# A hybrid attention and delta-rule layer on one core: the next block's inputs made ahead of the last projection, the delta rule's decode after the sixth head, two buffers for gate z

## The chip, the core and the metric

The kernel runs on one core of one Trainium2 chip. The metric is the device time of one execution in microseconds (us). Before the change it is 2385.31 us, the median of three runs (2379.32 to 2391.11). The profile is of one more execution, which took 2384.44 us; its span, from the first to the last instruction, is 2382.5 us.

Five engines work in parallel: TensorE (PE: matrix products and transposes; PEld is its loading of the stationary operand), VectorE (DVE), ScalarE (ACT), GpSimd (POOL) and SyncE (SP), which here only issues DMA transfers. ACT issues some transfers too. Each engine runs its instructions in the order in which they stand in its own queue, and an instruction that waits holds up everything behind it.

## The reference

One inference step of one layer, for two sequences: a prompt of 2048 rows of width 1024 with no past, and a sample of 8 sequences of 16 new rows with a cache of 512 past rows each. All in float32.

```
shift, scale, gate = split(silu(c) @ W_ada + b_ada)          # per sequence
h = LN0(x) * (1 + scale) + shift
[qA|kA|vA|gA | qkvB|zB|aB|bB | mA|mB] = h @ W_in             # widths 512 x 8, 4, 4, 1024, 1024
A = differential attention(4 heads, block-causal, relative bias) * silu(gA)
B = gated delta rule(4 heads, causal short conv on q/k/v, RMSNorm * silu(zB))
y = (sigmoid(mA) * (A @ W_pA) + sigmoid(mB) * (B @ W_pB)) @ W_out
x <- LN(alpha * x + gate * y) * ln_g + ln_b
```

Besides the new x it returns the new k and v rows, the last three rows ahead of the convolution and the final delta state (128 x 128 per head), for prompt and sample each. The sample's attention runs over its cache, its delta rule starts from a given state.

## The kernel before

**Phases.** The prompt is cut in four blocks of 512 rows. Phase one goes through 16 steps, one for each block b and head h; the sample's 128 rows ride along with block 0. Phase two then forms y and the new x in five blocks of 512, 512, 512, 384 and 256 rows, the last of which ends with the sample's 128. Between the phases A, B and the merge gates go through DRAM (`ascr`, `tscr`).

**Products in two halves.** Each float32 operand of the large products is split into a high part, a copy in the fast type, and a low part, the difference. A projection (`proj`, all products at L146) makes 128 columns of `h @ W_in` for a block as 24 products: eight slices k of the width with (whi, hhi), eight with (whi, hlo), eight with (wlo, hhi), into one PSUM tile of the pool `pp`, which has two buffers. A projection's result is taken out of `pp` by ACT, and by DVE for the gates, into tiles that often come from the pool `u` (six buffers); a merge gate's tile `tm` (L1378) goes to `tscr` by a transfer at L1380. The two halves of h fill the pool `h`, 16 buffers, so the next block's halves can only be written when the old block's last projection has read theirs. Weights come through the pool `w`, six buffers of 512 KB; they are split once, kept in DRAM (`wscr`) and loaded as pairs from then on, in the order of a list `order`. `split_n(n)` at the start of projection n also fetches n+1 and n+2.

**Four streams.** The program is written by four generators: `gates` (decays and betas of a block), `gdn` (the delta rule), `attention`, and `bulk` (the projections and, at the end, phase two). `plan` interleaves them by modelled due times: a generator gives up its turn with a delay, or with a key that another one must have signalled. After that `arrange` orders each engine's queue anew with a list scheduler over all instructions, with modelled durations. On TensorE products that read `hhi` or `hlo` are set back by 100 us (`AHEAD`), so that transposes, attention and delta rule go first when they are ready and projections fill the rest. Transfers on SP are ordered by when their readers are due; in the first 50 us of modelled TensorE time by their place in the program. Tiles of a pool are given out in program order.

**One step of bulk** is: three projections for attention (`a_proj`: k, q, v), the first merge gates, one more, the two gates of the head (`gate_proj`: g for attention, z for the delta rule, each in a pool with one buffer), the remaining merge gates, and the three delta-rule projections of the next step (`b_proj`: k, q, v with the convolution, into `kq`, two buffers, and `vT`). Gate z's buffer is freed by the last instruction of the head's delta rule (`norm_gate`, L885).

**The edge between blocks.** At the last head of a block, after `gate_proj`, `next_rows` (L404 on) loads the first 512 columns of the next 512 rows into pool `a`, and normalises them on DVE (L228). After the last merge gate `make_h` loads the other 512 columns into pool `u`, and `half_h` makes for each of the eight column slices four transposes into a `pp` tile (L150), the scaling into a `u` tile `h32` (ACT L421 or DVE L419 in turns), the high part on DVE (L401) and the low part on POOL (L402). The row statistics were made one head earlier by `block_stats`.

**The start.** `c` is loaded on SP; its tanh (L242), the transposes and the copy `cT` (L247) lead to `modulation(n)` for n = 0, 2, 1, 3. Each takes eight loads of `w_ada`, 256 KB apiece, on SP (L260) into pools `g` and `a`, eight float32 products into 32 columns each, a copy of the row on DVE (L264) and 16 small products. The x rows of block 0 and the sample, ten loads of 256 KB (L272), and the small set-up loads are issued by ACT.

**Decode and gate rows.** The sample's delta rule (`gdn_decode`) runs in the `gdn` stream after step `GD = (2, 2)` and takes ten tiles of the pool `g`, all of it. The sample's attention (`attn_decode`) runs four times, after the steps in `AD`, for two sequences each time; for each head it transposes 512 cached keys, copies them to `kTd` (pool `wt`, two buffers, L1306) and multiplies them with 32 stationary columns. `gate_rows`, the last third of `W_ada` (16 loads of 256 KB into `u`, at L260), stands at the end of bulk with the twelve small stores of the convolution's last rows (L1421), ahead of phase two, whose first loads are those of `ascr` (L1458) and whose first products are on `ahi` and `alo`.

Of the kernel before, what the change touches and what calls it, by code (L numbers as in the profile page):

```python
# [21 lines left out]
P = 128  # L22
# [3 lines left out]
BLK = 512  # L26
# [17 lines left out]
BUFS = dict(g=10, e=10, wt=2, ao=2, u=6, vT=2, z=1, gg=1, a=5, vv=4, k4=6, kq=2, xc=2, h=16, w=6)  # L44
# [52 lines left out]
GD = (2, 2)  # L97
# [9 lines left out]
GO = 1  # L107
LS = 2.0
# [5 lines left out]
def layer_kernel(  # L114
# [134 lines left out]
    def wide_c():  # L249
        cw_ = tl("wt", "cw_", (P, KD, 32))  # L250
        V.memset(cw_, 0.0)
        V.tensor_copy(cw_[:, :, 0:9], cT)
        return cw_
# [15 lines left out]
    for n in range(5):  # L269
        xt0.append([tl("e", "x0"), tl("e", "x1")])  # L270
        for u in range(2):
            nc.scalar.dma_start(xt0[n][u], rows_of(0, n)[:, u * 512:(u + 1) * 512])  # L272
# [34 lines left out]
    def setup_gates():  # L307
        wab = tl("ao", "wab", (P, KD, 8))
        nc.scalar.dma_start(wab, W[:, C_AB:C_AB + 8].rearrange("(k p) c -> p k c", p=P))
# [4 lines left out]
        nc.scalar.dma_start(nexa, a_log[0:1, :].to_broadcast([P, H]))  # L314
        S.activation(nexa, nexa, AF.Exp)
        V.tensor_scalar(nexa, nexa, -1.0, None, ALU.mult)
        nc.scalar.dma_start(dtb, dt_bias[0:1, :].to_broadcast([P, H]))
        cwr = tl("vv", "cwr", (P, P))[:48]
        nc.scalar.dma_start(cwr, conv_w[0].rearrange("j (n p) -> (j n) p", p=P))
# [4 lines left out]
        nc.scalar.dma_start(ng, Cd("neg"))  # L324
# [12 lines left out]
    def setup_attn():  # L337
        lamv = tl("vv", "lamv", (P, 4, 64))
        for n, a in enumerate((lam_q1, lam_k1, lam_q2, lam_k2)):
            nc.scalar.dma_start(lamv[:, n, :], a[0:1, :].to_broadcast([P, 64]))  # L340
# [11 lines left out]
        nc.scalar.dma_start(subw, subln_w.rearrange("o c -> c o"))  # L352
        V.tensor_scalar(subw, subw, 0.5 * (1.0 - LAM_INIT), None, ALU.mult)
        nc.scalar.dma_start(dnw, dn_norm_w.rearrange("o c -> c o"))
# [3 lines left out]
        nc.scalar.dma_start(rtab, rel_table)  # L358
        oh = tl("vv", "oh")[:32, :384]
        nc.scalar.dma_start(oh, Cd("onehot", 32))  # L360
# [43 lines left out]
    def next_rows(b, u):  # L404
        xs = [tl("au"[u], "xr") for _ in range(4)]
        for n in range(4):
            nc.sync.dma_start(xs[n], rows_of(b, n)[:, u * 512:(u + 1) * 512])
        for n in range(4):
            ln_apply(xs[n], *stats[b], n)
        return xs  # L410

    def half_h(b, u, hhi, hlo, xs):
        for k in range(4 * u, 4 * u + 4):
            pt = (ps_t, ps_pp)[k % 2]() if b == 0 else ps_pp()
# [3 lines left out]
            if k % 2 and b:  # L418
                V.tensor_scalar(h32, pt, modT[:, 8 + k, 0:1], modT[:, k, 0:1], ALU.mult, ALU.add)  # L419
            else:  # L420
                S.activation(h32, pt, AF.Identity, bias=modT[:, k, 0:1], scale=modT[:, 8 + k, 0:1])  # L421
            halves(h32, hhi[k][:, :512], hlo[k][:, :512], V if b == 0 and k % 2 else G)
# [46 lines left out]
    mcol = lambda ms: [(C_MA, C_MB)[w] + m * P for w, m in ms]  # L469
    order += bcol(0)  # L470
    for si, (b, h) in enumerate(steps):
        order += acol(h) + mcol(m_alpha[b, h] + m_beta[b, h][:GO]) + gcol(h) + mcol(m_beta[b, h][GO:])
        if si + 1 < len(steps):
            order += bcol(steps[si + 1][1])
# [21 lines left out]
    def fetch(n):  # L496
        if n < len(order) and n not in raws and n not in pairs:
            if order[n] in kept:
# [35 lines left out]
    def proj(b, evac):  # L534
# [5 lines left out]
        for si, (t0, n) in enumerate([(0, 320), (320, 320)] if b == 0 else [(0, 512)]):  # L540
            pa = ps_pp()
            q = 0
            for w_, x_ in ((whi, hhi), (whi, hlo), (wlo, hhi)):
                for k in range(KD):
                    T.matmul(pa[:, :n], lhsT=w_[:, k, :], rhs=x_[k][:, t0:t0 + n], start=(q == 0), stop=(q == 23))
                    q += 1
                    if q % 4 == 0 and q < 24:
                        yield
                    if q == 4 and si == 0:
# [1381 lines left out]
```

## Time and profile before

| | |
|---|---|
| median of three runs | 2385.31 us (2379.32 to 2391.11) |
| profiled execution, its own time | 2384.44 us |
| its span | 2382.5 us |
| PE busy | 2268.2 us, 95% |
| DVE, ACT, POOL busy | 1479.0, 857.6, 325.5 us |
| mean granted TensorE clock | 0.971 |
| DMA | 537.61 MB, 226 GB/s in the mean |

How to read it: busy time is the union of an engine's instructions. Where PE is granted half the clock, the same product is busy for about twice the time, so a stage loses time both by idle PE and by a clock below 1. "Idle before" with an arrow names what an instruction waited for, as far as semaphores show it.

### The profile page before, as it was taken

The page shows a single profiled execution, that of the slowest core. Times are in us where ns is not written, and L with a number is a line of the kernel's source. Part 1 is how long each engine was busy: PE and PEld are TensorE (multiplying, and loading weights), DVE is VectorE, ACT ScalarE, POOL GpSimd, SP SyncE. Part 2 cuts the span into 40 slices and gives each one's busy share as a digit, 9 for nine tenths or more (in the row PEclk, how much of TensorE's full clock was granted, in tenths as well). Part 3 has the DMA queues.
Part 4 walks back from the last instruction along what each step waited for, and adds up shares of the span by engine and source line. Part 5 has one row for each costly group of instructions (what it writes and reads, how often), then busy time and mean ns, then how long its engine had stood idle before and what let it go on. Part 6 is the DMA issues. An engine that isn't in the chain of part 4 may idle for free.

```text
span 2382.5 us, 41070 instructions
## 1 busy us (share of the span) xinstructions
PE 2268.2 (95%) x14228; PEld 1891.9 (79%) x14228; DVE 1479.0 (62%) x4765; ACT 857.6 (36%) x2604; POOL 325.5 (14%) x696
## 2 busy tenths in 40 slices
PE   4999999999999998999999989989999989999997
PEld 3899999967877786688888776877888766888886
DVE  4645566645655557476658784766777555467467
ACT  1344453533443424353534443534444431000000
POOL 0110120212020101120110022011012011110100
PEclk8899999999999998999999999999999988999999
DMA  8487787957676877375575856636364767797797
GB/s 280 120 268 219 234 267 225 293 176 215 201 249 194 272 229 267 113 231 179 187 239 184 266 174 201 235 97 211 125 216 149 232 202 265 251 358 270 285 376 271
DMA packets 314496, 537.61 MB, mean 226 GB/s; under 512 B 50903, under 2 KB 164079, under 8 KB 314288
## 3 DMA queue, kind: packets, MB, share of 16 engines
q1 hardware_dynamic: 299296, 511.99, 65.7%
q10 hardware_dynamic: 14992, 22.99, 2.8%
q8 instruction: 113, 1.85, 0.3%
q14 instruction: 95, 0.78, 0.1%
HBM read 381.73 MB, written 127.97 MB: 214 GB/s over the span
## 4 chain that ended last, share of the span: by engine, by line
PE 84%; DMA 8%; DVE 3%; SPq 2%; ACT 1%; issue 1%; POOL 0%; ACTq 0%; DVEq 0%; POOLq 0%
PE pp_t L146 51%; PE t_t L146 13%; PE g_t L146 8%; PE v_t L146 7%; PE t_t L150 4%; DMA ql<-lo 2%; DMA wa<-in_w_ada_dram 1%; PE g_t L150 1%; SPq L1061 1%; PE pp_t L150 1%; DMA kst<-lo 1%; DMA tscr<-tm 1%; DMA kscr<-kst 1%; DMA kld<-kscr 0%; DMA wlo<-wscr_m 0%
## 5 line engine op out<-in xcount | busy, mean ns | idle before, releaser
L146 PE MATMUL pp_t<-hhi,whi 128*128 128x512 f32 (+1 forms) x1920 | 467.0, 369 | 7.5 <-ACT tm L1378 3.3
L146 PE MATMUL pp_t<-hlo,whi 128*128 128x512 f32 (+1 forms) x1920 | 464.3, 367 | 0.0
L146 PE MATMUL pp_t<-hhi,wlo 128*128 128x512 f32 (+1 forms) x1920 | 462.3, 367 | 0.0
L146 PEld LDWEIGHTS pp_t<-hhi,whi 128*128 128x128 f32 x1920 | 328.2, 189 | 54.6 <-ACT xc L673 4.6
L146 PEld LDWEIGHTS pp_t<-hhi,wlo 128*128 128x128 f32 x1920 | 328.9, 189 | 44.8 <-issue 4.5
L146 PEld LDWEIGHTS pp_t<-hlo,whi 128*128 128x128 f32 x1920 | 327.0, 189 | 42.3 <-issue 3.9
L1175 DVE TENSOR_REDUCE nm<-t_t 128x1 f32<-128x512 f32 (+3 forms) x256 | 149.1, 591 | 124.6 <-PE t_t L146 121.0
L1182 ACT ACTIVATE e<-t_t,nm 128x512 f32<-128x512 f32 (+3 forms) x256 | 155.5, 610 | 91.4 <-DVE nm L1175 85.6
L1483 ACT ACTIVATE mhi<-th 128x512 fp32r<-128x512 f32 (+2 forms) x40 | 22.7, 568 | 334.5 <-DVE th L1481 129.0
L486 DVE TENSOR_TENSOR wlo<-wraw,whi 128x1024 fp32r<-128x1024 f32 (+1 forms) x80 | 80.6, 1010 | 76.0 <-PE pp_t L146 25.4
L655 DVE SCALAR_TENSOR_TENSOR y<-xc,cw,y 128x512 f32<-128x512 f32 x144 | 107.8, 748 | 1.0
L1216 DVE SCALAR_TENSOR_TENSOR e<-e,f 128x512 f32<-128x512 f32 (+3 forms) x196 | 106.7, 575 | 0.1
L146 PE MATMUL v_t<-vld,wt 128*128 128x128 f32 x768 | 105.0, 280 | 0.0
L146 PEld LDWEIGHTS v_t<-vld,wt 128*128 128x128 f32 x768 | 99.9, 195 | 5.1 <-ACT wt L1225 0.7
L1225 ACT COPY wt<-t_t 128x512 f32<-128x512 f32 (+2 forms) x96 | 51.1, 532 | 141.2 <-PE t_t L150 116.3
L402 POOL TENSOR_TENSOR lo<-k,hi 128x512 fp32r<-128x512 f32 x16 | 20.7, 1292 | 577.6 <-DVE hi L401 270.3
L770 POOL TENSOR_TENSOR tm<-lb,tb 32x15 f32<-32x15 f32 (+7 forms) x255 | 73.7, 289 | 167.8 <-DMA lb<-lscr 147.3
L150 PE MATMUL t_t<-cst,e 128*128 128x128 f32 x544 | 90.3, 277 | 4.5 <-DVE e L1216 4.5
L1462 POOL TENSOR_TENSOR alo<-araw,ahi 128x512 fp32r<-128x512 f32 (+2 forms) x40 | 46.1, 1164 | 324.1 <-DVE ahi L1460 213.8
L146 PE MATMUL t_t<-kld,qh 128*128 128x512 f32 x192 | 80.1, 423 | 8.9 <-DMA kld<-kscr 4.4
L772 POOL TENSOR_TENSOR tb<-tb,tm 32x15 f32<-32x15 f32 (+7 forms) x255 | 82.2, 322 | 19.5
L485 ACT ACTIVATE whi<-wraw 128x1024 fp32r<-128x1024 f32 (+1 forms) x80 | 70.0, 885 | 40.5 <-PE pp_t L146 38.9
(490 smaller groups left out, 4212.2 us busy)
## 6 DMA issues: line engine op xcount, KB each, us to landing
whi<-wscr SPq DMA_DIRECT2D x144, 512.0 KB
wlo<-wscr SPq DMA_DIRECT2D x144, 512.0 KB
wraw<-in_w_in_dram SPq DMA_DIRECT2D x48, 512.0 KB
wscr<-whi SPq DMA_DIRECT2D x48, 512.0 KB
wscr<-wlo SPq DMA_DIRECT2D x48, 512.0 KB
whi<-wscr_m SPq DMA_DIRECT2D x40, 512.0 KB
wlo<-wscr_m SPq DMA_DIRECT2D x40, 512.0 KB
woh<-wscr_o SPq DMA_DIRECT2D x36, 512.0 KB
```

What stands on the lines that cost most here:

```text
L146: return nc.tensor.matmul(out, lhsT=lhsT, rhs=rhs, **kw)
L150: return nc.tensor.transpose(out, in_, identity)
L485: S.activation(whi, r, AF.Copy)
L486: V.tensor_tensor(wlo, in0=r, in1=whi, op=ALU.subtract)
L655: V.scalar_tensor_tensor(y, in0=x_(j), scalar=taps(j), in1=y, op0=ALU.mult, op1=ALU.add)
L770: G.tensor_tensor(tm[:, :n, :j + 1], in0=bc(lb[:, j, j + 1:], j + 1), in1=tb[:, j:j + 1, :j + 1].to_broadcast([32, n, j + 1]), op=ALU.mult)
L772: G.tensor_tensor(tb[:, j + 1:, :j + 1], in0=tb[:, j + 1:, :j + 1], in1=tm[:, :n, :j + 1], op=ALU.subtract)
L1175: V.tensor_reduce(nm[:, c, n:n + 1], sp[:, sl], AX, ALU.max, negate=True)
L1182: S.activation(et[:, sl], src, AF.Exp, bias=nm[:, c, n:n + 1], accum_out=ls[:, c, n:n + 1])
L1216: V.scalar_tensor_tensor(e1[:, sl], in0=e2[:, sl], scalar=coef(1, n), in1=e1[:, sl], op0=ALU.mult, op1=ALU.add)
L1225: (S.copy if kb % 2 == 0 else V.tensor_copy)(wt[:, :w], pt[:, :w])
L1462: G.tensor_tensor(lo, in0=raw, in1=hi, op=ALU.subtract)
```

## The change

1. **The start.** The x loads move from ACT to SP, behind the weights of `modulation(0)`; the small set-up loads move from ACT to SP.
2. **The edge.** `next_h` takes the place of `next_rows` and of half of `make_h`. Ahead of the last merge-gate projections it loads eight column tiles of 512 rows x 128 columns (into five buffers of `a`, two of `xc`, one of `u`), normalises each in four pieces, transposes them, and lets ACT write the scaled result back into the same tile. `make_h`, after the last projection, only copies the high part (ACT) and subtracts (DVE). The first projection of all, and the last of each block and the first of the next, take their 24 products slice by slice.
3. **The gate rows.** `gate_rows` moves from the end of phase one to step (3, 1), between a merge gate and `gate_proj`. Its weights are four entries in `order`, each two tiles of 512 KB of the pool `w`, and it uses `pp`. The convolution's last rows stay at the end (`halo_rows`).
4. **The delta rule's decode** runs after step (1, 2) and no longer after (2, 2).
5. **Buffers.** `z` has two, `u` has five.
6. **The cache decode.** Keys of two heads are transposed and copied before the two products with them are issued, one behind the other.
7. `make_gates` issues its products with `hhi` and `hlo` slice by slice.

```diff
-BUFS = dict(g=10, e=10, wt=2, ao=2, u=6, vT=2, z=1, gg=1, a=5, ...)
+BUFS = dict(g=10, e=10, wt=2, ao=2, u=5, vT=2, z=2, gg=1, a=5, ...)
-GD = (2, 2)
+GD = (1, 2)
+GR = (3, 1)
...
-        for u in range(2):
-            nc.scalar.dma_start(xt0[n][u], rows_of(0, n)[:, u * 512:(u + 1) * 512])
+    def first_rows():
+        for n in range(5):
+            for u in range(2):
+                nc.sync.dma_start(xt0[n][u], rows_of(0, n)[:, u * 512:(u + 1) * 512])
...
-        nc.scalar.dma_start(wab, W[:, C_AB:C_AB + 8].rearrange("(k p) c -> p k c", p=P))
+        nc.sync.dma_start(wab, W[:, C_AB:C_AB + 8].rearrange("(k p) c -> p k c", p=P))
...
+    def next_h(b):
+        mv, r = stats[b]
+        xs = []
+        for k in range(KD):
+            x_ = tl("aaaaaxxu"[k].replace("x", "xc"), "xk")
+            nc.sync.dma_start(x_.rearrange("p (n c) -> p n c", c=P),
+                              x_rows[b * BLK:(b + 1) * BLK, k * P:(k + 1) * P].rearrange("(n p) c -> p n c", p=P))
+            xs.append(x_)
+        for k, x_ in enumerate(xs):
+            pt = ps_pp()
+            for n in range(4):
+                ln_apply(x_[:, n * P:(n + 1) * P], mv, r, n)
+                T.transpose(pt[:, n * P:(n + 1) * P], x_[:, n * P:(n + 1) * P], ident)
+            S.activation(x_, pt, AF.Identity, bias=modT[:, k, 0:1], scale=modT[:, 8 + k, 0:1])
+            yield HH
+        return xs
...
-    def make_h(b, x0):
-        hts[b] = new_h()
-        x1 = next_rows(b, 1)
-        yield from half_h(b, 0, *hts[b], x0)
-        yield from half_h(b, 1, *hts[b], x1)
+    def make_h(b, xs):
+        hts[b] = hhi, hlo = new_h()
+        for k in range(KD):
+            S.activation(hhi[k][:, :512], xs[k], AF.Copy)
+            V.tensor_tensor(hlo[k][:, :512], in0=xs[k], in1=hhi[k][:, :512], op=ALU.subtract)
...
+                pairs[n] = [tl("w", "wa2", (P, 2, 512)) for _ in range(2)]
+                for i, wa in enumerate(pairs[n]):
+                    nc.sync.dma_start(wa, w_ada[0][(k + 2 * i) * P:(k + 2 * i + 2) * P, (4 + u) * 512:(5 + u) * 512].rearrange("(k p) c -> p k c", p=P))
...
+            products = [(w_, x_, k) for w_, x_ in ((whi, hhi), (whi, hlo), (wlo, hhi)) for k in range(KD)]
+            if n0 in edges:
+                products = [products[8 * p + k] for k in range(KD) for p in range(3)]
...
-                kT = tl("wt", "kTd")
-                S.copy(kT, pt)
+                kTs.append(tl("wt", "kTd"))
+                S.copy(kTs[h], pt)
                 yield 1.0
-                q_ = qz[:, h, bi].rearrange("p c t -> p (c t)")
-                T.matmul(sp[32 * h:32 * h + 32, :], lhsT=q_, rhs=kT, start=True, stop=True)
+                if h % 2 == 0:
+                    continue
+                for g in (h - 1, h):
+                    q_ = qz[:, g, bi].rearrange("p c t -> p (c t)")
+                    T.matmul(sp[32 * g:32 * g + 32, :], lhsT=q_, rhs=kTs[g], start=True, stop=True)
...
+            if (b, h) == GR:
+                yield from gate_rows()
             yield from gate_proj(b, h)
             if h == H - 1 and b + 1 < NBLK:
-                x0 = next_rows(b + 1, 0)
+                xs = yield from next_h(b + 1)
...
-        yield from gate_rows()
+        yield from halo_rows()
```

More of the change, by code (lines that the diff above doesn't have):

```diff
@@ L351, in setup_attn @@
         V.tensor_tensor(lamd, in0=lamd, in1=C("cc")[:, 0:1], op=ALU.add)
-        nc.scalar.dma_start(subw, subln_w.rearrange("o c -> c o"))
+        nc.sync.dma_start(subw, subln_w.rearrange("o c -> c o"))
         V.tensor_scalar(subw, subw, 0.5 * (1.0 - LAM_INIT), None, ALU.mult)
-        nc.scalar.dma_start(dnw, dn_norm_w.rearrange("o c -> c o"))
+        nc.sync.dma_start(dnw, dn_norm_w.rearrange("o c -> c o"))
         V.tensor_scalar(dnw, dnw, 0.5, None, ALU.mult)
         rtab = small(H, "rtab", bufs=1)[:32]
-        nc.scalar.dma_start(rtab, rel_table)
+        nc.sync.dma_start(rtab, rel_table)
         oh = tl("vv", "oh")[:32, :384]
-        nc.scalar.dma_start(oh, Cd("onehot", 32))
+        nc.sync.dma_start(oh, Cd("onehot", 32))
         for h in range(H):
@@ L402, in halves @@
         eng.tensor_tensor(lo, in0=x_, in1=hi, op=ALU.subtract)
[L404 to L409, printed above, removed]
+    def next_h(b):
[13 more added lines that the diff above has]
+            yield HH
         return xs
@@ L417, in half_h @@
             h32 = tl("u", "h32")
[L418 to L422, printed above, removed]
+            S.activation(h32, pt, AF.Identity, bias=modT[:, k, 0:1], scale=modT[:, 8 + k, 0:1])
+            halves(h32, hhi[k][:, :512], hlo[k][:, :512], V if k % 2 else G)
             yield HH
@@ L469, in layer_kernel @@
     mcol = lambda ms: [(C_MA, C_MB)[w] + m * P for w, m in ms]
+    edges = {0}
     order += bcol(0)
     for si, (b, h) in enumerate(steps):
-        order += acol(h) + mcol(m_alpha[b, h] + m_beta[b, h][:GO]) + gcol(h) + mcol(m_beta[b, h][GO:])
+        order += acol(h) + mcol(m_alpha[b, h] + m_beta[b, h][:GO]) + [('gate', u, k) for u in range(2) for k in (0, 4) if (b, h) == GR] + gcol(h) + mcol(m_beta[b, h][GO:])
         if si + 1 < len(steps):
+            if h == H - 1:
+                edges |= {len(order) - 1, len(order)}
             order += bcol(steps[si + 1][1])
@@ L542, in proj @@
             q = 0
[L543 to L549, printed above, removed]
-                        split_n(n0 + 1)
-                    if q == 8:
-                        while later:
-                            later.pop(0)()
+            products = [(w_, x_, k) for w_, x_ in ((whi, hhi), (whi, hlo), (wlo, hhi)) for k in range(KD)]
+            if n0 in edges:
+                products = [products[8 * p + k] for k in range(KD) for p in range(3)]
+            for w_, x_, k in products:
+                T.matmul(pa[:, :n], lhsT=w_[:, k, :], rhs=x_[k][:, t0:t0 + n], start=(q == 0), stop=(q == 23))
+                q += 1
+                if q % 4 == 0 and q < 24:
+                    yield
+                if q == 4 and si == 0:
+                    split_n(n0 + 1)
+                if q == 8:
+                    while later:
+                        later.pop(0)()
             if n == 512:
@@ L1300, in attn_decode @@
             sp = ps_t()
+            kTs = []
             for h in range(H):
@@ L1421, in gate_rows @@
             nc.sync.dma_start(ncv_p[0, 0][:, n * P:(n + 1) * P], hl[3 * n:3 * n + 3, :])
-        cw_ = wide_c()
+        yield
+    def gate_rows():
+        cw_ = wide_c("u")
         for u in range(2):
+            pa = ps_pp()
+            for k0 in (0, 4):
+                n0 = cur[0]
+                cur[0] += 1
+                split_n(n0)
+                wa = pairs.pop(n0)
+                for k in range(k0, k0 + 4):
+                    g_ = slice(32 * (k - k0), 32 * (k - k0) + 32)
+                    T.matmul(pa[g_, :], lhsT=cw_[:, k, :], rhs=wa[(k - k0) // 2][:, k % 2], start=(k0 == 0), stop=(k0 == 4))
+                split_n(n0 + 1)
+                yield
+            row = tl("u", "row")
+            V.tensor_copy(row, pa)
+            yield
             ba = tl("u", "ba")[:9]
             nc.sync.dma_start(ba, b_ada[0:1, (4 + u) * 512:(5 + u) * 512].to_broadcast([9, 512]))
-            row = ada(cw_, 4 + u, "u")
             pt = ps_pp()
@@ L1562, in bulk @@
         modulation(0)
+        first_rows()
         first_norm()
@@ L1598, in bulk @@
                 if nb_ != b:
-                    yield from make_h(nb_, x0)
+                    yield from make_h(nb_, xs)
                 if si:
```

24 lines of the change are left out of this document (13 added, 11 removed).

## The prediction

> **What bounds the kernel.** First I read the page's summary: the span, the busy line and the clock line.
>
> ```profile
> span 2382.5 us, 41070 instructions
> PE 2268.2 (95%) x14228; PEld 1891.9 (79%) x14228; DVE 1479.0 (62%) x4765; ACT 857.6 (36%) x2604; POOL 325.5 (14%) x696
> PEclk8899999999999998999999999999999988999999
> ```
>
> TensorE is busy 95% of the span and no other engine comes near. Where it is always fed, only less TensorE work helps; time can also come from stages where it idles, or from the half clock that follows (the eights in the clock line). So the second view is the table of stretches, cut where the clock line dips. Columns: stretch, length, busy time and count of PE, PEld, DVE, ACT, POOL, granted clock, DMA share, GB/s.
>
> ```profile
> 0.00:26.00 26.00, 1.02 (x8) 0.93 (x8) 5.90 (x16) 2.39 (x3) 0.20 (x4) 1.00 0.86 271
> 26.00:50.00 24.00, 19.14 (x88) 11.44 (x89) 18.13 (x56) 2.70 (x6) 0.00 (x0) 0.79 0.80 252
> 50.00:76.00 26.00, 21.95 (x104) 13.55 (x104) 13.77 (x28) 5.68 (x8) 7.83 (x9) 0.63 0.48 163
> 508.00:537.00 29.00, 24.08 (x138) 16.16 (x137) 17.84 (x45) 11.70 (x32) 11.23 (x10) 0.88 0.27 92
> 936.00:961.00 25.00, 16.30 (x70) 8.68 (x69) 13.86 (x30) 5.73 (x9) 13.64 (x24) 0.66 0.39 119
> 1398.00:1424.00 26.00, 19.26 (x99) 13.39 (x97) 20.59 (x60) 9.21 (x31) 11.27 (x9) 0.80 0.45 144
> 1596.00:1620.00 24.00, 15.04 (x63) 10.97 (x62) 14.07 (x56) 8.05 (x31) 0.00 (x0) 0.72 0.21 71
> 1935.00:1985.00 50.00, 36.08 (x245) 21.18 (x244) 19.69 (x55) 9.03 (x32) 4.09 (x5) 0.70 0.62 206
> ```
>
> I put a stage's loss at its length less PE busy, plus length times (1 - clock). That gives at most 25.0 + 9.9 + 13.7 = 48.6 us at the start; 8.4, 17.2 and 11.9 (37.5) at the three edges between blocks; 15.7 at 1596; and 28.9 before phase two. The change touches all of these.
>
> **The start.** Third I followed the chain of waits and the ACT and PE timelines of the first 80 us.
>
> ```profile
> 1.49 4.61 DMA cst<-in_const_dram
> 0.73 6.41 ACTq L272 DMA_DIRECT2D x<-in_x_prompt_dram  x8
> 17.04 1.05 ACT L242 ACTIVATE cth<-call 9x1024 f32<-9x1024 f32 x1
> 25.95 0.23 ACT L247 ACTIVATE cT<-t_t 128x72 f32<-128x72 f32 x1 [7.86 <-DMA subw<-in_subln_w_dram]
> 26.47 3.42 PE L146 MATMUL g_t<-wa,cw__113 128*32 128x512 f32 x16 [6.05 <-DVE cw__113 L252]
> 62.44 2.51 PE L146 MATMUL g_t<-wa,cw__113 128*32 128x512 f32 x16
> 76.38 19.50 PE pp_t L146 x121
> 5.00:10.00 5.00, 0.00 (x0) 0.00 (x0) 1.32 (x3) 0.00 (x0) 0.00 (x0) 1.00 1.04 384
> ```
>
> The tanh of c waits behind ACT's own loads until 17.04, and cT behind more of them until 25.95, though the constants had landed at 6.1. So the first modulation product starts at 26.47 and the last at 62.44, and the projections run from 76.38. The change moves ten x loads, behind modulation 0's weights, and thirteen small loads to SP. Then transfers set the end: 32 wa loads and ten of x, tiles of 128 x 512 floats or 256 KB each, and two raw weights of 512 KB are 12.1 MB, 31 us at 384 GB/s. Begun at 2 us, with some 2 us for the small loads, they land near 35.5, not before 62.44: an estimate of -27. At the other end SP serves alone: the 23 moved issues at 6.41/8 = 0.80 us take 18 us, leaving -9. Pool buffers could hold the wa loads too. I take -20, nearer the transfers, as the DMA share falls to 0.48 in the third stretch. Nothing hides this time: the projections are TensorE's main work.
>
> The Trainium skill (DMA: Bandwidth & Descriptors, Issuing engines are not separate DMA queues) says that SP and ACT feed the same 16 DMA engines, so that spreading loads over both saves issue time alone. This speaks against the move: by the rule its effect is the issue time lost on SP, -9; by the row of 384 GB/s, with ACT held until 25.95, it is -27.
>
> **The edges.** Now the next block's h is made after the old block's last projection. `make_h` fetches the second half of x into `u` buffers, normalises, transposes through `pp`, and POOL makes `hlo`.
>
> ```profile
> 938.20 6.37 DMA tscr<-tm
> L150 PE MATMUL pp_t<-cst,xr 128*128 128x128 f32 x96 | 20.1, 346 | 15.2 <-DVE h L419 12.0 <-ACT h L421 2.0 <-ACT tm L1378 0.9
> L228 DVE TENSOR_SCALAR xr<-xr,mv,rs 128x512 f32<-128x512 f32 x24 | 14.5, 616 | 1.1 <-DMA xr<-in_x_prompt_dram 1.1
> L1215 DVE TENSOR_SCALAR e<-e,f 128x128 f32<-128x128 f32 x40 | 10.4, 280 | 0.0
> L419 DVE TENSOR_SCALAR h<-pp_t,modT 128x512 f32<-128x512 f32 x12 | 9.7, 804 | 11.2 <-DMA tscr<-tm 6.1 <-PE pp_t L150 3.3 <-POOL hlo L402 1.2
> L401 DVE CAST hhi<-h 128x512 fp32r<-128x512 f32 x32 | 18.3, 574 | 5.0 <-ACT h L421 4.8
> L402 DVE TENSOR_TENSOR hlo<-h,hhi x4: 679/820/959, 59.6 to 76.6; 128x512 fp32r<-128x512 f32 x4
> ```
>
> No projection runs for 23 to 29 us at an edge; the chain shows h waiting 6.37 us for a `u` buffer that a `tm` store held. After the change eight column tiles are loaded early, normalised, transposed and scaled in place ahead of the last projection; only two conversions per tile remain, and products ordered by k let them run under the neighbouring projections. Per tile DVE now does four pieces of 0.280 us, 1.12 us, and eight tiles through two `pp` buffers take 9 us. With today's loss rate at the edges (37.5 of 80 us) that leaves 4.2 us each, 13 in all: -24. DVE gains work: 32 x 0.280 + 8 x 0.82 = 15.5 us an edge against 8 x 0.616 + 4 x 0.804 + 8 x 0.574 = 12.7, and ACT takes over half the scaling and all of the first conversions. At 14 to 21 us of DVE and 6 to 12 of ACT in these stretches both have room; if DVE were last everywhere the surplus alone would be +8. I charge 2. Taken: -22, bounds -37 to +8. The loads move earlier into `a` and `xc` buffers that stand empty after the head's own projections, and carry the same bytes.
>
> **The gate z and the decode.**
>
> ```profile
> 1319.00 0.75 DVE L885 SCALAR_TENSOR_TENSOR go<-g_t,dnw,z 128x512 f32<-128x512 f32 x1 [0.99 <-PE g_t L150]
> 1534.90 0.75 DVE L885 SCALAR_TENSOR_TENSOR go<-g_t,dnw,d 128x512 f32<-128x512 f32 x1 [0.18 <-PE g_t L150]
> 1542.13 0.60 ACT L695 ACTIVATE th<-pp_t 128x512 f32<-128x512 f32 x1 [0.37 <-PE pp_t L146]
> 1604.30 0.69 DVE L657 SCALAR_TENSOR_TENSOR kq<-th,y 128x512 f32<-128x512 f32 x1 [1.07 <-PE g_t L146]
> 1614.37 0.75 DVE L885 SCALAR_TENSOR_TENSOR go<-g_t,dnw,z 128x512 f32<-128x512 f32 x1 [1.21 <-PE g_t L150]
> 1615.15 0.69 DVE L697 SCALAR_TENSOR_TENSOR z<-th,pp_t 128x512 f32<-128x512 f32 x1
> 1709.07 0.75 DVE L885 SCALAR_TENSOR_TENSOR go<-g_t,dnw,z 128x512 f32<-128x512 f32 x1 [0.25 <-PE g_t L150]
> ```
>
> The delta stream leaves head (2,2) at 1319.0, spends until 1534.9 on the decode and finishes (2,3) at 1614.4. Gate z of (3,0) was projected by 1542.1, but its one buffer is free only then, so it keeps one of two `pp` buffers for 73 us and the projections stop at 1596. A second z buffer ends that: -13 of 15.7 (0 to -15.7). The decode after (1,2) moves the 216 us of lag, with its loads and stores on SP, to blocks 1 and 2. `kq` still has two buffers, and at 1604.30 it too waited for the delta stream, so one such stall can come near (2,1). With z free, the next head's attention can run under it: 0 to +15.7, taken +6.
>
> **The gate rows.**
>
> ```profile
> 1932.38 0.63 PE L146 MATMUL pp_t<-hhi,wlo 128*128 128x512 f32 x2
> 1935.19 6.65 SPq L1421 DMA_DIRECT2D out_dram<-hl  x12
> 1974.84 3.36 SPq L1458 DMA_DIRECT2D araw<-ascr  x5
> 1980.93 0.77 PE L146 MATMUL pp_t<-ahi,whi 128*128 128x512 f32 x1
> 1680.00:1740.00 60.00, 59.31 (x354) 51.10 (x355) 41.79 (x134) 25.12 (x82) 6.72 (x15) 1.00 0.51 148
> ```
>
> The last projection ends at 1933.0; on SP twelve small stores and sixteen wa loads stand ahead of phase two's first load at 1974.84, and products follow 6.1 us later. Without the wa loads I expect products at 1933.0 + 6.65 + 6.1 = 1946. The 11 us up to there keep their share of the loss, 6.4 us; with 3 for filling the first tiles: -19 (-8, if SP's order stays poor, to -28.9). The wa loads, 4.2 MB, now stand among block 3's weights. At 148 GB/s for a share of 0.51 the pipe gives 290, so they take 14.5 us; the weights behind them come late by up to that, while attention is TensorE's cover. 0 to +14.5; taken +6.
>
> **The cache decode's pairs and `u`.**
>
> ```profile
> L146 PE MATMUL t_t<-kTd,keep 128*32 128x512 f32 x64 | 34.4, 632 | 1.3 <-DVE keep L1292 1.2
> 53.21 1.15 PE L146 MATMUL g_t<-wa,cw__113 128*32 128x512 f32 x8
> ```
>
> Each score product into 32 columns is two instructions alone, 34.4/32 = 1.07 us. Four such products issued together take 1.15. Sixteen pairs save up to 16 us; a quarter of them stands at edges, where TensorE isn't the limit: -11 (0 to -16). One `u` buffer fewer: two waits like the 6.37 us would cost 12; taken +4 (0 to +12). The pairing of the small gate products (hi and lo by k) changes only their order: 0.
>
> **Sum.** -20 - 22 - 13 + 6 - 19 + 6 - 11 + 4 = -69. The profiled execution took 2384.4 us, 1.9 outside its span and within 0.9 of the median 2385.3. So 2315.
>
> **Rivals.** A: the outer ends gain, the middle gives back. Freed idle at the edges and at 1596 returns as waits for the delta stream: only -20 and -19 remain, 2345. For it: go to go at 1614.4 and 1709.1 is 95 us, hardly faster than a head of projections. Against: PE is busy 59.31 of 60 at 1680 in spite of that lag.
>
> B: it doesn't do what it says. If two `pp` buffers, not the chain to h, make the edge (the wait on `tm` speaks for it), and SP's order holds start and end, then -9 - 8 - 11 + 16 = -12: 2372 to 2375, no change that can be seen. Against: h waits 12.0 us on DVE and 0.9 on `tm` in the grouped row.
>
> C: slower. The decode's lag starves `kq` at every head from (2,1) to (3,3). Seven stalls of 15.7 us are 110; with the +6 already charged, 2315 + 104 = 2419. It decides from 75/7 = 11 us a head. For it: `kq` waited at 1604. Against: after 1620 the same lag cost nothing.
>
> **Numbers.** Forecast 0.63 (2285 to 2345), A 0.21, B 0.09, C 0.07. About 0.5%, 12 us, can be told from no change. Faster takes the forecast and A, 0.84; same is B; slower is C. The range 2285 to 2373 leaves out C, part of B and a little below.
>
> **What would show it.** Start: the first projection before 60 us. Edges: stretches without projections under 12 us, clock near 1. Gate: z written soon after its projection, no stop at block 3's second head. End: products on ahi within 15 us of the last projection. Pairs: about 18 us less in the kTd group. Wrong would be a first projection after 70 us, idle TensorE near (2,1) or around the wa loads of block 3, or ACT waiting on `u`.

## The result and the profile after

The changed kernel takes 2323.36 us in the median of four runs (2316.22 to 2324.34), beside 2386.1 us for the kernel before on the same chip: a ratio of 0.9732, 95% interval 0.9701 to 0.9764. That is 64 us or 2.7% (56 to 71 us) faster. The profiled execution took 2316.22 us, the fastest of the four; its span is 2314.4 us. One execution of the experiments, of 7862 us, was far slower than all others of its kernel and is left out of its median.

The page's summary, clock line included:

```profile
span 2314.4 us, 41136 instructions
PE 2234.2 (97%) x14228; PEld 1878.5 (81%) x14228; DVE 1467.0 (63%) x4825; ACT 880.2 (38%) x2640; POOL 296.0 (13%) x672
PEclk8999999989999999999999999999999999999999
```

To see where the time came from, both spans are cut at the same marks: the first projection product, the first product of the gates in blocks 1, 2 and 3, the last projection, the first product on `ahi`, the end. Columns: stretch, length, busy time and count of PE, PEld, DVE, ACT, POOL, granted clock, DMA share, GB/s. Before:

```profile
0.00:81.00 81.00, 46.95 (x218) 28.52 (x219) 39.89 (x103) 10.76 (x16) 9.95 (x16) 0.79 0.67 214
81.00:531.50 450.50, 442.19 (x3443) 423.00 (x3442) 255.44 (x836) 203.60 (x600) 62.05 (x150) 0.99 0.76 237
531.50:960.10 428.60, 414.36 (x2524) 330.32 (x2522) 257.65 (x950) 172.17 (x541) 60.68 (x144) 0.98 0.71 226
960.10:1415.10 455.00, 444.55 (x2848) 363.34 (x2847) 314.45 (x1095) 202.64 (x633) 55.32 (x129) 0.99 0.63 203
1415.10:1933.00 517.90, 501.52 (x3138) 403.59 (x3139) 344.34 (x1086) 231.42 (x727) 89.35 (x212) 0.98 0.57 180
1933.00:1980.90 47.90, 34.03 (x248) 19.97 (x247) 19.64 (x55) 9.84 (x31) 2.01 (x8) 0.73 0.63 212
1980.90:2382.50 401.60, 384.63 (x1820) 323.19 (x1819) 247.56 (x646) 27.18 (x57) 46.11 (x40) 0.98 0.84 301
```

After:

```profile
0.00:67.00 67.00, 49.35 (x217) 25.92 (x217) 39.44 (x103) 10.77 (x16) 10.03 (x16) 0.80 0.79 259
67.00:512.80 445.80, 438.24 (x3406) 421.67 (x3407) 252.74 (x839) 202.60 (x592) 54.85 (x144) 0.97 0.76 236
512.80:932.60 419.80, 408.36 (x2577) 330.84 (x2575) 278.60 (x1087) 188.90 (x585) 42.35 (x114) 1.00 0.74 237
932.60:1378.60 446.00, 441.49 (x2778) 360.21 (x2777) 296.27 (x1027) 202.93 (x626) 75.99 (x182) 0.99 0.67 212
1378.60:1896.40 517.80, 507.88 (x3428) 412.70 (x3426) 350.29 (x1130) 249.18 (x774) 64.91 (x177) 1.00 0.59 187
1896.40:1906.50 10.10, 3.59 (x16) 3.15 (x16) 6.70 (x23) 2.00 (x8) 0.00 (x0) 0.83 0.85 294
1906.50:2314.40 407.90, 385.25 (x1812) 323.97 (x1812) 242.99 (x623) 23.86 (x44) 47.83 (x40) 0.98 0.84 297
```

As in the prediction a stage's loss is its length less PE busy, plus length times (1 - clock). The clock has two digits, so the loss of a long row is good to some 2 us. How good a sum is shows in a kernel that does the same work as the one before, with the decode alone moved: span less loss is 2212 us there and 2202 before, so a sum is good to some 10 us. In the last three columns stand kernels of the experiments, cut at their own marks.

| loss, us | before | after | decode back at (2,2) | one z buffer | both back, six u |
|---|---|---|---|---|---|
| start | 51.1 | 31.0 | 32.4 | 31.4 | 33.6 |
| block 0 | 12.8 | 20.9 | 18.0 | 16.3 | 14.3 |
| block 1 | 22.8 | 11.4 | 8.9 | 13.4 | 23.2 |
| block 2 | 15.0 | 9.0 | 15.0 | **36.0** | 4.2 |
| block 3 | 26.7 | 9.9 | **41.2** | 10.6 | **52.4** |
| to the first product on `ahi` | 26.8 | 8.2 | 5.5 | 5.2 | 6.1 |
| phase two | 25.0 | 30.8 | 44.5 | 35.2 | 28.1 |
| sum | 180.2 | 121.2 | 165.5 | 148.1 | 161.9 |

Of the 68 us by which the spans differ, 59 are loss: 20 at the start, 17 in block 3, 19 ahead of phase two, 17 in blocks 1 and 2 with the edges at their ends, less 8 in block 0 and 6 in phase two. The other 9 come out as less work for TensorE, which is no more than the sums are good to.

The signs that the prediction named: products on `ahi` come 10.2 us after the last projection (within 15: right), gate z is written soon after its projection (right), the first projection starts at 67.0 (not before 60: wrong, though not past 70), the `kTd` group is 16.6 us smaller (about 18: right). At the edges the longest stretches without a projection are 14.7 us at 478 (under 12: wrong), then 8.9 and 6.3 (right); the clock there is 0.72, 0.91 and 0.90, not near 1. At block 3's second head the projections still stop, for 32 us from 1567 (no stop there: wrong), now for the gate rows; TensorE idles 5.6 us of that stretch.

### The profile page after: what moved, and what is told of

Read it like the earlier page. It is cut to its first block, busy times and chain, and to the rows that moved or that the text cites. A ratio compares the mean times of both kernels' runs of the same rounds, so it can differ in the third digit from the quotient of the medians.

```text
span 2314.4 us, 41136 instructions
## 1 busy us (share of the span) xinstructions
PE 2234.2 (97%) x14228; PEld 1878.5 (81%) x14228; DVE 1467.0 (63%) x4825; ACT 880.2 (38%) x2640; POOL 296.0 (13%) x672
## 4 chain that ended last, share of the span: by engine, by line
PE 84%; DMA 6%; DVE 5%; issue 2%; ACT 1%; SPq 1%; POOL 0%; ACTq 0%; DVEq 0%; POOLq 0%
PE pp_t L147 52%; PE t_t L147 12%; PE g_t L147 7%; PE v_t L147 7%; PE t_t L151 3%; DMA kld<-kscr 1%; PE g_t L151 1%; PE pp_t L151 1%; SPq L1084 1%; DMA wol<-wscr_o 1%; DMA xk<-in_x_prompt_dram 1%; DMA th<-tscr 1%; DMA wa<-in_w_ada_dram 0%; DMA kst<-lo 0%; DMA araw<-ascr 0%
## 5 line engine op out<-in xcount | busy, mean ns | idle before, releaser
L147 PE MATMUL pp_t<-hhi,whi 128*128 128x512 f32 (+1 forms) x1920 | 478.0, 369 | 7.0 <-ACT tm L1405 5.6
L147 PE MATMUL pp_t<-hlo,whi 128*128 128x512 f32 (+1 forms) x1920 | 473.9, 368 | 0.0
L147 PE MATMUL pp_t<-hhi,wlo 128*128 128x512 f32 (+1 forms) x1920 | 468.9, 366 | 0.0
L1526 ACT ACTIVATE mhi<-th 128x512 fp32r<-128x512 f32 (+2 forms) x40 | 22.7, 568 | 350.2 <-DVE th L1524 167.9
L1248 ACT COPY wt<-t_t 128x512 f32<-128x512 f32 (+2 forms) x96 | 51.1, 532 | 110.5 <-PE t_t L151 99.7
L147 PE MATMUL pp_t<-ahi,whi 128*128 128x512 f32 (+2 forms) x320 | 78.7, 363 | 8.1 <-DVE ahi L1503 5.0
```

What stands on the lines that cost most here:

```text
L147: return nc.tensor.matmul(out, lhsT=lhsT, rhs=rhs, **kw)
L1248: (S.copy if kb % 2 == 0 else V.tensor_copy)(wt[:, :w], pt[:, :w])
```

## The experiments

Every kernel was timed beside the kernel before on its chip. A difference from the changed kernel is the difference of the two ratios times 2386 us; with the intervals of both it is good to about 9 us where nothing else is said. All compute the whole layer.

### The start taken back

```diff
-                nc.sync.dma_start(xt0[n][u], rows_of(0, n)[:, u * 512:(u + 1) * 512])
+                nc.scalar.dma_start(xt0[n][u], rows_of(0, n)[:, u * 512:(u + 1) * 512])
...  (ahead of modulation(0) again; the thirteen small loads too)
```

> The changed kernel with part 1 taken back: the ten x loads and the thirteen small loads are issued by ACT again, everything else as after the change (2323 us). Theory (the start gains what the tanh of c no longer waits for): the first projection product, at 67.0 us after the change and 81.0 before, goes back to about 81, and the time to 2323 + 14 to 17 = 2337 to 2340. Rival (only the issue time on SP counts, 9 us, the transfers share one set of DMA engines anyway): 2332 or less, the first projection near 76.

Measured: 2329.1 us, ratio 0.9762 (0.9745 to 0.9779), 7 us slower. The first projection is at 77.9. Its start loses 46.9 us and not 31.0, but block 0 then loses 16.2 in place of 20.9, and block 1 loses 22.7 in place of 11.4, for which the edit gives no reason. So the stage was worth 16 us in the trace and about 7 in the time; by the time alone the rival isn't excluded. What the edit put in the place of the old wait is seen in the changed kernel itself. The tanh of c no longer waits (ACT); then come on SP the first and the last of the thirteen small loads and the weights behind them, and the stretches there:

```profile
4.34 1.05 ACT L243 ACTIVATE cth<-call 9x1024 f32<-9x1024 f32 x1
```

```profile
19.51 0.42 SPq L313 DMA_DIRECT2D wab<-in_w_in_dram  x1
26.47 0.42 SPq L364 DMA_DIRECT2D oh<-in_const_dram  x1
27.31 3.04 SPq L261 DMA_DIRECT2D wa<-in_w_ada_dram  x6
```

```profile
21.00:24.00 3.00, 2.88 (x12) 0.54 (x10) 2.69 (x12) 0.00 (x0) 0.00 (x0) 0.68 0.88 231
24.00:27.00 3.00, 3.00 (x22) 1.69 (x16) 2.37 (x10) 0.42 (x2) 0.00 (x0) 1.00 0.11 28
27.00:30.00 3.00, 2.91 (x16) 2.54 (x17) 1.62 (x7) 0.20 (x1) 0.00 (x0) 0.96 0.72 179
```

For 7.4 us SP issues loads of 0.5 to 64 KB at some 0.57 us each, and the 16 DMA engines run nearly dry: a share of 0.11 at 24 to 27. Whether this is what now sets the first projection is not shown here; the last experiment moves these loads.

### The edge taken back

```diff
-                xs = yield from next_h(b + 1)
+                x0 = next_rows(b + 1, 0)
...  (old half_h and make_h; edges = {0})
```

> The changed kernel with part 2 taken back: next_rows and the old make_h, products at the edges in the old order. Theory (the inputs made ahead fill the edges): the three stretches lose 37.5 us again instead of some 22 by length less busy plus clock, so 16 us or more: 2339, up to 2345 by the prediction's -22. Rival (two pp buffers make the edge): 8 us or less, 2331 at most.

Measured: 2339.23 us, ratio 0.9817 (0.9797 to 0.9836), 20 us slower, as the theory said. Without the new edge no projection runs for 31.1, 32.3 and 29.3 us at the three block changes. In the kernel before, counted the same way, it is 27.9, 25.8 and 20.4 us: the old edge takes its tiles from `u`, which has five buffers here and had six. So part of the 20 us can be the price of that tile on the old edge. The same places of the changed kernel:

```profile
478.00:499.00 21.00, 18.73 (x225) 12.81 (x225) 7.56 (x29) 10.71 (x24) 0.39 (x2) 0.72 0.62 196
914.00:934.00 20.00, 14.35 (x84) 9.03 (x82) 13.88 (x59) 11.21 (x30) 1.48 (x4) 0.91 0.78 244
1367.00:1400.00 33.00, 30.10 (x262) 21.89 (x261) 19.18 (x55) 17.18 (x43) 0.00 (x0) 0.90 0.42 139
```

They lose 8.1, 7.5 and 6.2 us, beside 8.4, 17.2 and 11.9 before. The first edge gained nothing: PE is busy there, but with short products, and is granted 0.72. Its half clock lasts until 504; from 478 to 505 it loses 10.9 us, where the kernel with the edge taken back loses 5.6 (487 to 521). So there the new edge costs.

### The gate rows taken back

```diff
-            if (b, h) == GR:
-                yield from gate_rows()
...
-        yield from halo_rows()
+        yield from gate_rows()      # as before, with the twelve small stores
```

> The changed kernel with part 3 taken back: the gate rows' sixteen loads and products stand at the end of phase one again, and none of their 4 MB is loaded in block 3. Theory (the prediction's terms -19 at the end and +6 in block 3): the gap of 32.6 us without a projection at 1567 closes and gives back 5 to 6 us, the end loses 19 more: 2336. Rival 1 (the loads in block 3 cost nothing, attention covers them): 2342 or more. Rival 2 (the loads starve the weights by their whole 14.5 us): 2327 or less.

Measured: 2342.07 us, ratio 0.9816 (0.9796 to 0.9835), 20 us slower: rival 1. Products on `ahi` come 43.8 us after the last projection and not 10.2. Block 3 without the gate rows' loads loses 9.0 us, with them 9.9: in sum their 4 MB cost nothing that the trace shows. The projections do stop for 32 us in the changed kernel, but TensorE has attention and the delta rule, and idles only 5.6 of the 35 us from 1565, at the full clock:

```profile
1565.08 1.97 PE L147 MATMUL pp_t<-hhi,wlo 128*128 128x512 f32 x8
1568.83 1.92 PE L147 MATMUL pp_t<-wa,cw__19903 128*32 128x512 f32 x16
1587.85 1.92 PE L147 MATMUL pp_t<-wa,cw__19903 128*32 128x512 f32 x16
1599.24 0.97 PE L147 MATMUL pp_t<-hhi,whi 128*128 128x512 f32 x3 [0.77 <-DVE ba L1472]
```

### The decode taken back, with two z buffers

```diff
-GD = (1, 2)
+GD = (2, 2)
```

> The changed kernel with the delta rule's decode after step (2,2) again, two buffers for z kept. Theory (the second z buffer alone ends the hold of 73 us, the move of the decode costs up to 6): 2317 to 2323, no stop of the projections over 10 us at block 3's second head but that of the gate rows. Rival (the decode's lag, not z, made the stop, through kq's two buffers; moving the decode is what ended it): a stop of about 15 us at block 3's first or second head again, now together with the gate rows' loads, and 2335 to 2345.

Measured: 2356.73 us, ratio 0.9873 (0.9848 to 0.9898), **34 us slower**. The theory fell, and with it the prediction's step that a second z buffer leaves no stop in block 3. Block 3 of this kernel, and 20 us of the stop:

```profile
1380.40:1910.90 530.50, 510.53 (x3168) 409.36 (x3167) 348.64 (x1089) 234.78 (x726) 78.29 (x184) 0.96 0.58 186
```

```profile
1580.00:1600.00 20.00, 14.48 (x81) 10.80 (x76) 6.17 (x20) 5.78 (x21) 0.00 (x0) 0.54 0.06 23
```

Its PE, DVE and ACT, one behind the other:

```profile
1577.22 1.19 PE L147 MATMUL pp_t<-hhi,wlo 128*128 128x512 f32 x4
1597.10 1.22 PE L147 MATMUL g_t<-state,kq 128*128 128x128 f32 x4
1600.50 1.65 PE L147 MATMUL pp_t<-hhi,whi 128*128 128x512 f32 x3 [0.35 <-ACT tm L1405]
```

```profile
1598.35 0.69 DVE L680 SCALAR_TENSOR_TENSOR kq<-th,y 128x512 f32<-128x512 f32 x1 [0.88 <-PE g_t L147]
```

```profile
1599.08 0.63 ACT L679 ACTIVATE th<-y 128x512 f32<-128x512 f32 x1 [0.77 <-DVE kq L680]
1599.87 1.07 ACT L1405 ACTIVATE tm<-pp_t 128x512 f32<-128x512 f32 x2
```

The last product that reads the old `kq` runs at 1597, DVE writes the next `kq` at 1598.35, ACT's `th` of the same convolution follows, and behind it in ACT's queue the two evacuations of `pp` that let projections start at 1600.5. For 22 us TensorE had only the delta rule's chain of short products, at a clock of 0.54 in the 20 us shown: 5.5 us of these are idle and 9.2 are lost by the clock. The gate rows make a second stop right behind, 23.4 us from 1612.3; the stretches 1576 to 1602 and 1602 to 1637 lose 17.2 and 9.8 us.

In the kernel before it was z that ended the stop, as the prediction read it. `kq` is written at 1604.30 there, but the projections go on only when z, written at 1615.15, has given its `pp` buffer to the transposes of k:

```profile
1616.89 0.49 PE L150 MATMUL pp_t<-cst,k 128*128 128x128 f32 x3
1618.60 0.60 ACT L1067 ACTIVATE kr<-pp_t 128x512 f32<-128x512 f32 x1 [1.33 <-PE pp_t L150]
1619.25 2.11 PE L146 MATMUL pp_t<-hhi,whi 128*128 128x512 f32 x8 [0.69 <-ACT kr L1067]
```

So with two z buffers that wait is gone, and the wait for `kq`, which had ended 11 us earlier and was hidden behind it, stops the projections in its place. And the last head's delta rule ends at 2004, 93 us after the last projection, where it ends at 1890 in the changed kernel; phase two is 435 us long and not 408.

### One buffer for z, with u at five and at six

```diff
-BUFS = dict(g=10, e=10, wt=2, ao=2, u=5, vT=2, z=2, ...)
+BUFS = dict(g=10, e=10, wt=2, ao=2, u=5, vT=2, z=1, ...)   # first kernel
+BUFS = dict(g=10, e=10, wt=2, ao=2, u=6, vT=2, z=1, ...)   # second kernel
```

> The changed kernel with one buffer for gate z again, u left at five. Theory (the stop before was the delta stream's lag through kq; with the decode after (1,2) the delta rule is no longer a head late in block 3, so z has nothing to wait for): within 4 us of the changed kernel's 2323. Rival (the second z buffer is worth the 13 us of the prediction): 2336.

> The changed kernel with one buffer for gate z and six for u, as before. Against the same kernel with u at five this is the price of one common tile. Prediction's +4 (up to 12): 4 us faster than that one. Rival (the tile fewer costs nothing): the same within 3 us.

Measured: 2346.77 us, ratio 0.9853 (0.9831 to 0.9875), 29 us slower; and 2334.16 us, ratio 0.9798 (0.9776 to 0.982), 16 us slower. The theory formed from the run before fell too: with the decode after (1,2) the second z buffer is worth a lot. Its wait has only moved, from block 3 to block 2, and again the projections go on only after z:

```profile
933.00:1420.30 487.30, 465.94 (x2901) 374.52 (x2900) 305.63 (x1059) 214.10 (x663) 73.58 (x180) 0.97 0.61 193
```

```profile
1113.63 0.69 DVE L680 SCALAR_TENSOR_TENSOR kq<-th,y 128x512 f32<-128x512 f32 x1 [0.88 <-PE g_t L147]
1123.23 0.75 DVE L908 SCALAR_TENSOR_TENSOR go<-g_t,dnw,z 128x512 f32<-128x512 f32 x1 [1.21 <-PE g_t L151]
1124.02 0.69 DVE L720 SCALAR_TENSOR_TENSOR z<-th,pp_t 128x512 f32<-128x512 f32 x1
```

No projection runs from 1099.6 for 29.7 us; z is written 5 us before its end. The changed kernel at the same place, DVE and PE:

```profile
1056.47 0.68 DVE L720 SCALAR_TENSOR_TENSOR z<-th,pp_t 128x512 f32<-128x512 f32 x1
1117.07 0.69 DVE L680 SCALAR_TENSOR_TENSOR kq<-th,y 128x512 f32<-128x512 f32 x1
1130.87 0.76 DVE L908 SCALAR_TENSOR_TENSOR go<-g_t,dnw,z 128x512 f32<-128x512 f32 x1 [0.24 <-PE g_t L151]
```

```profile
1116.79 1.86 PE L147 MATMUL pp_t<-hhi,whi 128*128 128x512 f32 x7
```

`kq` comes as late as in the other kernel, 1117 and 1114, and `go`, which reads the older z and so frees its buffer, later still, at 1130.9; but the next z was written at 1056 and its `pp` buffer given back, and projections run through.

The two kernels differ by one tile of `u`: 12.6 us (by the ratios 13, good to 7), where the prediction had 4 and a bound of 12. Part of it lies in phase two, whose `araw` loads go into `u`. The group of the `ahi` casts, after its bar the busy time, the mean and the idle time ahead, in the changed kernel, with one z and five u, with one z and six u:

```profile
L1503 DVE CAST ahi<-araw 128x512 fp32r<-128x512 f32 (+2 forms) x40 | 20.3, 518 | 38.6 <-DMA araw<-ascr 38.6
```

```profile
L1503 DVE CAST ahi<-araw 128x512 fp32r<-128x512 f32 (+2 forms) x40 | 20.3, 510 | 43.4 <-DMA araw<-ascr 43.0
```

```profile
L1503 DVE CAST ahi<-araw 128x512 fp32r<-128x512 f32 (+2 forms) x40 | 24.5, 624 | 31.0 <-DMA araw<-ascr 31.0
```

### The decode's move alone

The kernel before with one edit:

```diff
-GD = (2, 2)
+GD = (1, 2)
```

> The kernel before with one edit alone: the delta rule's decode runs after step (1,2) in place of (2,2); z keeps one buffer, u six. Theory (the lag after (2,2) is what stops block 3 and what is left over in phase two): 25 to 34 us faster than before, 2352 to 2361, and no gap of the projections over 10 us at 1596. Rival (the move pays only with the second z buffer): 2372 or more. The prediction's own step, taken alone: 6 us slower than before, 2392.

Measured: 2389.64 us, ratio 1.0027 (1.0012 to 1.0042): 6 us **slower**, and the theory of a gain missed. The prediction's own step is met to the microsecond, but by luck: its +6 was meant for the move with a second z buffer in place. Its blocks 2 and 3:

```profile
961.80:1461.40 499.60, 475.31 (x2920) 380.59 (x2918) 315.57 (x1061) 208.30 (x657) 78.66 (x185) 0.97 0.60 190
1461.40:1937.60 476.20, 472.32 (x3139) 386.49 (x3140) 323.82 (x1023) 224.62 (x691) 69.51 (x179) 1.00 0.58 184
```

Block 3 loses 3.9 us in place of 26.7, block 2 loses 39.3 in place of 15.0: the stop is carried from one block to the other (31.8 us without a projection from 1123.3, ended by z at 1150.9). On the kernel before, the move with one z buffer pays nothing, as the rival has it; in the changed kernel it does pay, as the next run shows.

### All three of that trade taken back

```diff
-BUFS = dict(g=10, e=10, wt=2, ao=2, u=5, vT=2, z=2, ...)
-GD = (1, 2)
+BUFS = dict(g=10, e=10, wt=2, ao=2, u=6, vT=2, z=1, ...)
+GD = (2, 2)
```

> The changed kernel with three edits of one trade taken back together: decode after step (2,2), one buffer for z, six for u. These are the prediction's terms -13, +6 and +4, together -3. Prediction: 2326. Theory formed from the single undos (each of the two edits alone meets the other's wait, so that together they remove one stop of the projections and not two, about the 15 us at 1596 before, and the tile of u costs 11): block 3 stops once at about 1580, the end is late by the lag, 2323 + 25 to 35 for the decode's lag, less 11 for the tile: 2337 to 2347. Rival (the single losses of 34 and 11 add): 2365 or more.

Measured: 2353.09 us, ratio 0.9878 (0.9852 to 0.9904), 35 us slower. So the losses of 34 and 16 don't add, but it is more than the theory gave.

```profile
1371.80:1930.20 558.40, 528.38 (x3266) 421.72 (x3266) 356.76 (x1144) 245.60 (x771) 89.39 (x213) 0.96 0.57 184
```

Block 3 loses 52.4 us here and lost 26.7 in the kernel before, which has the same decode place and the same buffers. No projection runs for 43.9 us from 1548.7, beside 22.9 at 1596 before, and again z ends it: `kq` is written at 1577.2, z at 1588.0, the projections go on at 1592.7. Block 3 begins 43 us earlier than in the kernel before (1371.8, beside 1415.1), but the delta rule ends head (2,3) only 27 us earlier (1587.2, beside 1614.4): the projections come to the same wait with a larger lead. The gate rows are not in this stop; theirs is a later one, 16.1 us from 1632.9. Four corners, all with the other parts of the change in place:

| | decode after (1,2) | decode after (2,2) |
|---|---|---|
| two z, five u | 0.9732 | 0.9873 |
| one z, six u | 0.9798 | 0.9878 |

So in the changed kernel the move is worth 34 us with two z buffers and 19 with one. The second z buffer, with the tile of `u` that it costs, is worth 16 us after the move and 1 without it. Each is good to 8 to 10 us.

### The pairs taken back

```diff
-                for g in (h - 1, h):
...
+                T.matmul(sp[32 * h:32 * h + 32, :], lhsT=q_, rhs=kT, start=True, stop=True)
```

> The changed kernel with the cache decode's score products one by one again, each behind its own copy of kTd. The kTd group is 17.8 us after the change and 34.4 before. Theory (TensorE is the limit where they run, but for a quarter at the edges): 11 us slower, up to 16: 2334 to 2339. Rival (the pairs run under waits that stay): 2328 or less.

Measured: 2343.15 us, ratio 0.9832 (0.9807 to 0.9856), 24 us slower. The group in the changed kernel and in this one:

```profile
L147 PE MATMUL t_t<-kTd,keep 128*32 128x512 f32 x64 | 17.8, 633 | 0.0
```

```profile
L147 PE MATMUL t_t<-kTd,keep 128*32 128x512 f32 x64 | 32.6, 605 | 2.2 <-DVE keep L1315 2.2
```

It grows by 14.8 us, and the losses of the two kernels come out the same (121.0 and 121.2 by the seven rows, good to some 10). So it is TensorE work on the path, with nothing of it hidden, and the prediction's discount of a quarter was wrong. The rest of the 24 lies within the interval.

### Half of th2 out of u

```diff
-                    th = tl("u", "th2")[:, :n]
+                    th = tl(("u", "vT")[w], "th2")[:, :n]
```

> The changed kernel with half of phase two's th2 tiles taken from vT, which is empty by then, and no longer from u. Theory (half of the price of the missing u tile lies in phase two, where ahi waits 38.6 us for araw against 26.4 before and 31.0 with six tiles): phase two, 407.9 us from the first product on ahi, becomes 402 to 404, and the time 2317 to 2320. Rival (the price lies in phase one): no change, 2323.

Measured: 2315.73 us (2312.97 to 2316.65), ratio 0.9721 (0.9696 to 0.9746). The cast's wait for `araw` falls from 38.6 to 31.0 us, that of six u tiles, but phase two only from 407.9 to 405.1. It is the fastest kernel of all, by 3 us, which isn't told apart from the changed kernel by the intervals.

### The gate rows split over two steps

```diff
-GR = (3, 1)
+GR = [(3, 0), (3, 2)]        # gate_rows(u), one half in each
...  (dU and dones by nc.sync; th2 as above)
```

> The changed kernel with the th2 tiles as in the other kernel, the two halves of the gate rows at steps (3,0) and (3,2) in place of both at (3,1), and the loads of dU and dones issued by SP in place of ACT. Theory: -4 to -6 for th2, up to -6 for the 32.6 us gap of the projections around the gate rows' loads (it splits in two that attention covers), -2.8 for ACT's wait for an ao buffer ahead of the last tiles of h at the start: 2309 to 2313. Rival (the loads cost the same wherever they stand): 2315 to 2318.

Measured: 2327.51 us, ratio 0.9773 (0.9748 to 0.9798): 12 us slower than with th2 alone. The stretch after the first new place, this kernel and then the changed one:

```profile
1455.00:1505.00 50.00, 45.69 (x329) 32.96 (x328) 9.88 (x29) 9.32 (x26) 0.53 (x3) 0.86 0.77 262
```

```profile
1455.00:1505.00 50.00, 50.00 (x376) 39.85 (x375) 13.97 (x38) 11.80 (x31) 0.24 (x2) 1.00 0.81 268
```

The longest gap of the projections in block 3 is 9.7 us now and not 32, but the block loses 27.0 us in place of 9.9. At step (3,0) the DMA engines are already full (a share of 1.04 from 1440 to 1460 in the changed kernel), with the cache decode's keys and values, attention's and the weights. That 2 MB of gate rows on top of these cost the 11 us lost in this stretch (4.3 by idling, 7.0 by the clock) fits; it wasn't tested by moving the other loads.

### The small loads last

```diff
-        setup_gates()
-        setup_attn()
         modulation(1)
...
         fetch(0)
+        setup_gates()
+        setup_attn()
...  (dU and dones by nc.sync; th2 as above)
```

> The changed kernel with half of th2 in vT, dU and dones issued by SP, and the thirteen small set-up loads moved behind the last modulation's weights in the program. After the change they stand on SP from 19.1 to 26.4 us, and the transfers fall to a share of 0.10 between 24 and 27. Theory (the issue time of the small loads on SP is what the start still loses): the weights come about 6 us earlier, the first projection at 60 to 62 in place of 66.7, the time 2315.7 - 5 = 2309 to 2312. Rival (the first gates and the bias tables, now loaded last, hold up the first block by as much): 2315 to 2320.

Measured: 2322.66 us in the median of five, ratio 0.9768 (0.9739 to 0.9797), by the ratios 11 us slower than with th2 alone (good to 9): the rival, and worse. Six weights are issued from 19.4 us and no longer from 27.3, but the last nine only at 35.8 again, behind the small loads, and the products of the bias tables now stand ahead of the last modulation: the first projection is at 69.3. Why those nine weights did not go ahead of the small loads (pool buffers, or SP's order) wasn't settled.

## Why the prediction was right, and where it wasn't

**The time** (2315 forecast, 2323 measured) is right, and the forecast's case with it; but its terms are so only in part. Taken back one at a time the parts cost 7, 20, 20, 35 (z, decode and u together) and 24 us: 106 us, where the terms add up to 69 and the whole change brought 64. So the terms were 37 us too small in sum, and the parts overlap by 42. That these two nearly cancel is luck.

**Start, -20: over-sized.** The first projection came 14 us earlier, not 20 or more, and taking the edit back costs 7 us. The step that failed is that transfers would set the end: what the change takes off ACT's queue (the tanh runs at 4.34 and not at 17.04) it puts on SP's, where thirteen loads leave the transfers at a share of 0.11. The other end of the bounds, -9 by SP's issue time, fits the time; the 14 us of the trace lie between the two. The rule of the Trainium skill that was cited there (DMA: Bandwidth & Descriptors, Issuing engines are not separate DMA queues) leads to that same -9, and the time agrees: 7 us, good to 9. What holds the first projection now stays open, as moving the thirteen loads behind the weights did not bring it earlier (69.3).

**Edges, -22: right** (20 measured, part of it perhaps the old edge's need of a sixth `u` tile). The gain is at the second and third edge. The DVE-bound 9 us were not met at the first, which now loses more than with the edit taken back: the trace shows hardly any idle time to fill there, but short products at half the clock.

**Gate z -13 and the decode +6: wrong as two terms.** The reading of the stop at 1596 was right: z ended it. What failed is the sentence that a second z buffer ends the stop: with the decode at (2,2) the buffer and its tile are worth 1 us, as the wait for `kq`, quoted as a second and smaller matter, then stops the projections for 22 us. The forecast price of the move "with z free", +6, failed as well: with z free the move brings 34 us. The three edits together (z, decode, u) were forecast at -3 and are worth -35 in the changed kernel. Which corner stops where is shown, and which wait ends each stop can be read from the traces. Why a `kq` that comes late stops two z buffers in block 3 and doesn't in block 2 is read from one place of each trace (ACT's evacuations of `pp` behind the convolution's `th`) and wasn't tested by a third `kq` buffer.

**Gate rows, -19 at the end and +6 in block 3.** The first is right: the loss ahead of phase two fell by 18.6 us. The second is 0 in sum, as attention covered most of it; the rows split over two other steps cost 12 us, so it is a matter of place.

**Pairs, -11: under-sized.** 15 us of work, nothing of it hidden. **u, +4: under-sized.** 13 us, good to 7; the row of the wait on a `tm` store was too far from phase two's `araw`, where part of it came up.

**The rivals.** A (the middle gives the gain back) didn't come: blocks 1 to 3 lose 30 us and lost 65. B's small size of the edge (8 us) is not what the run without the new edge shows (20, good to 9), though with five u. C's mechanism, the wait for `kq`, is real with the decode at (2,2) and two z buffers, but it stops the projections once and not at seven heads; in the changed kernel `kq` comes late in block 2 (1117) and nothing stops.

**The terms don't add.** Each was measured with the others in place. The run with z, decode and u taken back shows one way in which they overlap: what the projections gain ahead of block 3 makes their wait for the delta rule there longer (43.9 us, beside 22.9 before).

## What to carry to other kernels

When two waits end close together, the one that ends last stops the work, and the other is hidden behind it until that one is taken away: here z ended the stops with one buffer, and `kq` the one with two. So the buffer alone brought 1 us and the move alone, on the kernel before, a loss of 6. And a gain ahead of a wait on another stream can only lengthen that wait. A buffer given to one pool is paid by another, and the price is to be looked for at every user of that pool, the far ones too (13 us for one tile, part of it in phase two). A transfer moved to the head of the line is free only where the pipe has room; look at the DMA share of the very stretch.

## What the runs showed of the hardware

A run of small loads on one queue left the transfers nearly empty: thirteen loads at 0.57 us each, and the share of the 16 DMA engines was 0.11 from 24 to 27 us, though weights of 256 KB stood right behind them.

A stop of the projections can be paid twice. With TensorE busy 14.48 of 20 us on the delta rule's short products the granted clock was 0.54, and block 3 of the kernel with the decode at (2,2) lost 20 us by idling and 21 by the clock. Yet in the changed kernel's stop for the gate rows, with attention on TensorE (busy 29.4 of 35 us from 1565), the granted clock stayed at 1.00.

It doesn't take a long idle stretch: between 1570 and 1612 of the kernel with the decode at (2,2) TensorE never idles for more than 1.1 us, and still the granted clock is half from 1581.8 to 1605.7. At the first edge of the changed kernel it is busy for 16.4 of 17 us from 487 to 504, mostly with short products, at a granted clock of 0.50. Which property of these products the clock follows wasn't tested.
